# Relative-position-bias softmax: stores on ScalarE's queue, single-row first loads, one last store

## The chip, the cores and the metric

The kernel runs on one core of a Trainium2 chip. The metric is device time in microseconds (us) of one execution; the median of three runs before the change is 1330.56 us (1330.31 to 1331.54). The profile is of one further execution, taken by the hardware profiler.

## The reference

The input is a tensor of logits of shape (2, 8, 2112, 2112) in fp32 and, per head, a table of 33 biases. Each logit gets the bias of its clipped relative position, and each row goes through a softmax:

```python
rel = pos[:, None] - pos[None, :]
rel_clipped = np.clip(rel, -16, 16) + 16
logits = logits + rel_bias[:, rel_clipped][None]
logits = logits - logits.max(axis=-1, keepdims=True)
exp = np.exp(logits)
return exp / exp.sum(axis=-1, keepdims=True)
```

Input and output have 285.5 MB each, and every element is read once and written once.

## The kernel before

A row of the softmax has S = 2112 elements (8448 bytes). Rows are dealt to the 128 partitions so that one partition holds 33 consecutive rows of one head: 64 blocks of 33 rows make the 2112 rows of a head, and two heads fill the 128 partitions. Inside a partition the bias of a row is a window into one strip `F` of 2144 values, shifted by one place from row to row. `strip(k)` builds `F` from the bias table for a pair of heads.

The outer loop `k` runs over K = 4 pairs of heads. Inside it there are 12 chunks: two batches, each cut into chunks of 6, 5, 6, 5, 6 and 5 rows per partition. That makes 48 chunks over the whole run. Four buffers `X[0]` to `X[3]` (`NBUF`) of up to six rows hold chunks in turn, so chunk n uses buffer n mod 4, and it is loaded, computed in place, and stored from there.

The engines go through a chunk like this:

- `add` on VectorE (L167): per row, one instruction adds the strip's window and gives the negated row maximum. It waits for the chunk's load (`ld[b]`).
- `exps` on ScalarE (L175): per row, the exponential with its row sum.
- `scale`: VectorE takes the reciprocals of the sums (L183) and scales the first three rows (`DV = 3`, L187), counting `scaled`.
- `scale_rest` on ScalarE (L192) scales the other two or three rows, counting `scaledA`.

VectorE and ScalarE each run a hardware loop over `k` with the 12 chunks written out.

All transfers of logits and results are issued by SyncE (SP). `load` (L87) fetches a whole chunk, and `store` (L95) first waits until the chunk is scaled. The first four loads are issued at the start; from then on `turn` gives the order:

```python
store(k + n // NT, n % NT)
take(nc.sync, st[(n - 1) % NBUF], 16)
load(k + (n + 3) // NT, (n + 3) % NT)
```

So SP issues store n, waits until store n-1 has landed, and then issues load n+3 into the buffer that became free. All of these stand in one queue, loads and stores in turn. The last chunk is stored in two parts: its first three rows, which VectorE scales, and then its last two. The bias table (132 KB, L103) is the only transfer on ScalarE's queue; `strip` needs it.

Of the kernel before, what the change touches and what calls it, by code (L numbers as in the profile page):

```python
# [11 lines left out]
ENG = mybir.EngineType  # L12
# [3 lines left out]
def kernel(  # L16
# [6 lines left out]
    nc = tc.nc  # L23
    P = 128
    B, H, S, S2 = logits.shape
# [4 lines left out]
    K = H // 2  # L30
# [3 lines left out]
    NBUF = 4  # L34
    SIZES = [6, 5, 6, 5, 6, 5]
# [3 lines left out]
    CH = [(b, sum(SIZES[:i]), r) for b in range(B) for i, r in enumerate(SIZES)]  # L39
    NT = len(CH)  # L40
# [3 lines left out]
    X = [io.tile([P, R * S], FP32, tag=f"X{b}", name=f"X{b}") for b in range(NBUF)]  # L44
# [14 lines left out]
    def rows(t, k, m, s0, n):  # L59

        b, j, r = CH[m]
        return bass.AP(
            tensor=t.tensor,
            offset=t.offset + (b * H * S + j + s0) * S + k * (2 * S * S),
            ap=[[W * S, P], [1, n * S]],
        )

    with tc.tile_critical(no_gpsimd_drain=True):
        ld = [nc.alloc_semaphore(f"ld{b}") for b in range(NBUF)]
        st = [nc.alloc_semaphore(f"st{b}") for b in range(NBUF)]  # L70
        added = nc.alloc_semaphore("added")
        expd = nc.alloc_semaphore("expd")
        scaled = nc.alloc_semaphore("scaled")
        scaledA = nc.alloc_semaphore("scaledA")
        inv = nc.alloc_semaphore("inv")
        invA = nc.alloc_semaphore("invA")
        rb = nc.alloc_semaphore("rb")
        idx = nc.alloc_semaphore("idx")
        dve = nc.alloc_semaphore("dve")

        def take(eng, sem, n):
            eng.wait_ge(sem, n).then_inc(sem, -n)  # L82


        def load(k, m):
            b, r = m % NBUF, CH[m][2]
            nc.sync.dma_start(out=X[b][:, 0 : r * S], in_=rows(logits, k, m, 0, r)).then_inc(ld[b], 16)  # L87

        def store(k, m, s0=0, n=None):
            b, n = m % NBUF, n or CH[m][2]  # L90
            if s0 < DV:
                take(nc.sync, scaled, DV)
            if s0 + n > DV:
                take(nc.sync, scaledA, s0 + n - DV)
            nc.sync.dma_start(  # L95
                out=rows(out, k, m, s0, n), in_=X[b][:, s0 * S : (s0 + n) * S]
            ).then_inc(st[b], 16)

        for m in range(NBUF):
            load(0, m)  # L100

        rbB = view(F, 0, [[1, H * W]])
# [1 line left out]
            out=rbB,  # L104
            in_=bass.AP(tensor=rel_bias.tensor, offset=rel_bias.offset, ap=[[0, P], [1, H * W]]),
# [7 lines left out]
        v = nc.vector  # L113
# [23 lines left out]
        def strip(k):  # L137

            then(v.tensor_copy(out=rbK[:, :], in_=rbP[:, bass.ds(k, 1), :]))  # L139
            settle()  # L140
            low, high = rbK[:, W - 1 : W], rbK[:, 0:1]
            blocks = view(F, MR, [[W, NB], [1, W]])
            then(v.tensor_tensor(out=blocks, in0=view(eq, 0, [[1, NB], [0, W]]),  # L143
                                 in1=view(rbK, W - 1, [[0, NB], [-1, W]]), op=ALU.mult))
            then(v.tensor_scalar(out=rest, in0=lt, scalar1=low, scalar2=None, op0=ALU.mult))  # L145
            then(v.tensor_copy(out=F[:, 0:MR], in_=low.to_broadcast([P, MR])))  # L146
            then(v.tensor_copy(out=F[:, FW - MR : FW], in_=high.to_broadcast([P, MR])))  # L147
            settle()
            then(v.scalar_tensor_tensor(out=rest, in0=gt, scalar=high, in1=rest, op0=ALU.mult, op1=ALU.add))  # L149
            settle()  # L150
            then(v.tensor_tensor(out=blocks, in0=blocks, in1=view(rest, 0, [[1, NB], [0, W]]), op=ALU.add))  # L151
            settle()

        def row(m, i):
            return X[m % NBUF][:, i * S : (i + 1) * S]

        def col(t, m, i, n=1):
            c = m % NBUF * R + i
            return t[:, c : c + n]

        DV = 3

        def add(m):
            take(v, ld[m % NBUF], 16)
            j, r = CH[m][1:]
            for i in range(r):
                v.tensor_tensor_reduce(  # L167
                    out=row(m, i), in0=row(m, i), in1=F[:, W - 1 - j - i : W - 1 - j - i + S],
                    scale=-1.0, scalar=BIG, op0=ALU.add, op1=ALU.min, accum_out=col(nmax, m, i),
                ).then_inc(added, 1)  # L170

        def exps(m):
            for i in range(CH[m][2]):
                take(nc.scalar, added, 1)
                nc.scalar.activation(  # L175
                    out=row(m, i), in_=row(m, i), func=ACTF.Exp, scale=-1.0, bias=col(nmax, m, i),
                    accum_out=col(tot, m, i),
                ).then_inc(expd, 1)

        def scale(m):  # L180
            r = CH[m][2]
            take(v, expd, r)
            v.reciprocal(out=col(rec, m, 0, r), in_=col(tot, m, 0, r)).then_inc(inv, 1)  # L183
            v.wait_ge(inv, 1).then_inc(inv, -1)  # L184
            v.sem_inc(invA, 1)
            for i in range(DV):
                v.tensor_scalar_mul(out=row(m, i), in0=row(m, i), scalar1=col(rec, m, i)).then_inc(scaled, 1)  # L187

        def scale_rest(m):
            take(nc.scalar, invA, 1)  # L190
            for i in range(DV, CH[m][2]):
                nc.scalar.activation(  # L192
                    out=row(m, i), in_=row(m, i), func=ACTF.Copy, scale=col(rec, m, i),
                ).then_inc(scaledA, 1)

        with nc.Fori(0, K, 1, engines=[ENG.DVE]) as k:
            strip(k)
            for m in range(NT):
                add(m)
                scale(m)  # L200
        with nc.Fori(0, K, 1, engines=[ENG.Activation]):  # L201
            for m in range(NT):
                exps(m)
                scale_rest(m)

        def turn(k, first, stop):
            for n in range(first, stop):
                store(k + n // NT, n % NT)  # L210
                take(nc.sync, st[(n - 1) % NBUF], 16)
                load(k + (n + 3) // NT, (n + 3) % NT)

        store(0, 0)
        with nc.Fori(0, K - 1, 1, engines=[ENG.SP]) as k:
            turn(k, 1, NT + 1)
        turn(K - 1, 1, NT - 3)
        for m in range(NT - 3, NT - 1):
            store(K - 1, m)
        r = CH[NT - 1][2]  # L220
        store(K - 1, NT - 1, 0, DV)
        store(K - 1, NT - 1, DV, r - DV)
        for b in range(NBUF):
            take(nc.sync, st[b], 32 if b == (NT - 1) % NBUF else 16)


# [28 lines left out]
```

## Time and profile before

| | |
|---|---|
| median of three runs | 1330.56 us |
| profiled execution | 1330.28 us, span 1328.5 us |
| VectorE busy | 818.9 us (62%) |
| ScalarE busy | 808.8 us (61%) |
| moved by DMA | 571.13 MB, 430 GB/s over the span |
| share of 16 DMA engines' time on SP's queue | 99.7% |
| median from issue to landing, load of six / five rows | 39.7 / 42.1 us |
| median from issue to landing, store of six / five rows | 46.9 / 48.6 us |

The span runs from the first to the last recorded instruction. GB/s counts what the DMA engines moved in either direction, and a DMA share of 1.00 means that all 16 engines had a packet in hand all the time. A packet is counted where it falls, so rates of short windows waver by some per cent. "SPq" and "ACTq" are the sequencers of SyncE and ScalarE, on which the DMA issues stand; they are not counted as busy time.

### The profile page before, as it was taken

The numbers are of one execution on the slowest core, as the hardware profiler recorded it, in microseconds if no ns is written. First come the engines' busy times: TensorE is split into PE (matmuls) and PEld (weight loads), VectorE is DVE, ScalarE is ACT, GpSimd is POOL, SyncE is SP. The second block draws the span as 40 slices with busy tenths as digits, with TensorE's granted clock in tenths as the row PEclk, the third lists the DMA queues.
The fourth block names the chain that finished last, engine by engine and source line by source line (L and its number), as shares of the span: only waits on it lengthen the run. The fifth ranks groups of instructions, "written<-read, shape, count | busy, mean of one in ns | idle before, by whom it ended". The sixth has DMA issues, their size and how long they took to land. (4 is left out here: it accounts for less than half of the span.)

```text
span 1328.5 us, 2379 instructions
## 1 busy us (share of the span) xinstructions
DVE 818.9 (62%) x753; ACT 808.8 (61%) x652; POOL 0.6 (0%) x6
## 2 busy tenths in 40 slices
DVE  4885665557755566555866466664676547665572
ACT  2895575655756557555675566764667646675472
POOL 0000000000000000000000000000000000000000
DMA  9999999999999999999999999999999999999998
GB/s 390 436 426 427 427 434 429 430 429 439 432 435 429 431 442 428 439 430 429 440 431 438 428 432 435 437 436 428 430 431 445 429 424 436 434 431 430 435 433 371
DMA packets 14117, 571.13 MB, mean 430 GB/s; under 512 B 1568, under 2 KB 1696, under 8 KB 1696
## 3 DMA queue, kind: packets, MB, share of 16 engines
q1 hardware_dynamic: 13968, 570.96, 99.7%
q10 hardware_dynamic: 144, 0.14, 0.0%
q14 instruction: 5, 0.04, 0.0%
HBM read 285.61 MB, written 285.47 MB: 430 GB/s over the span
## 5 line engine op out<-in xcount | busy, mean ns | idle before, releaser
L167 DVE CUSTOM_DVE_ANT_0 X<-X,F 128x2112 f32<-128x2112 f32 x264 | 605.5, 2354 | 340.1 <-DVEq L82 340.1
L175 ACT ACTIVATE X<-X,nmax 128x2112 f32<-128x2112 f32 x264 | 542.2, 2054 | 407.4 <-ACTq L82 381.6
L192 ACT ACTIVATE X<-X,rec 128x2112 f32<-128x2112 f32 x120 | 238.8, 2046 | 29.0 <-ACTq L82 29.0
L187 DVE TENSOR_SCALAR X<-X,rec 128x2112 f32<-128x2112 f32 x144 | 181.4, 1316 | 12.4 <-DVEq L184 12.4
L183 DVE RECIPROCAL rec<-tot 128x6 f32<-128x6 f32 (+1 forms) x48 | 9.1, 190 | 116.1 <-DVEq L82 116.1
L175 ACT ACTIVATION_READ_ACCUMULATOR X<-X,nmax 128x1 f32 x264 | 49.2, 186 | 0.0
L175 ACT ACT_TABLE_LOAD x4 | 5.1, 1283 | 60.7 <-ACTq L82 60.7
L167 DVE DVE_READ_ACCUMULATOR2_ANT nmax<- 128x1 f32 x264 | 21.8, 83 | 0.0
L151 DVE TENSOR_TENSOR F<-F,rest 128x2112 f32<-128x2112 f32 x4 | 9.4, 2359 | 0.6
L143 DVE TENSOR_TENSOR F<-Z,rbK 128x2112 f32<-128x2112 f32 x4 | 9.4, 2358 | 0.6
L134 DVE COPY rbP<-F 64x132 f32<-64x132 f32 x2 | 0.4, 224 | 14.5 <-DMA F<-in_rel_bias_dram 14.4
L149 DVE SCALAR_TENSOR_TENSOR rest<-Z,rbK,rest 128x64 f32<-128x64 f32 x4 | 1.1, 284 | 0.6 <-DVEq L82 0.2
L128 DVE TENSOR_SCALAR Z<-F 128x64 f32<-128x64 f32 x3 | 0.5, 221 | 1.5 <-POOL F L108 1.5
L145 DVE TENSOR_SCALAR rest<-Z,rbK 128x64 f32<-128x64 f32 x4 | 1.1, 275 | 0.0
L139 DVE COPY rbK<-rbP 128x33 f32 x4 | 0.7, 176 | 0.3 <-DVEq L82 0.3
L147 DVE COPY F<-rbK 128x16 f32<-128x16 f32 x4 | 0.7, 167 | 0.0
L146 DVE COPY F<-rbK 128x16 f32<-128x16 f32 x4 | 0.7, 164 | 0.0
L108 POOL IOTA F<- 64x64 f32 x2 | 0.4, 178 | 0.7 <-PEq L250 0.6
L239 POOL MEMSET const-bfloat16-1.0<- 128x1 bf16 x1 | 0.1, 101 | 0.0
L239 POOL MEMSET const-float32-0.0<- 128x1 f32 x1 | 0.1, 98 | 0.2 <-issue 0.2
L239 POOL MEMSET const-float32-1.0<- 128x1 f32 x1 | 0.1, 98 | 0.0
L239 POOL MEMSET const-uint8-127<- 128x1 uint8 x1 | 0.1, 98 | 0.0
## 6 DMA issues: line engine op xcount, KB each, us to landing
X<-in_logits_dram SPq DMA_DIRECT2D x24, 6336.0 KB, 39.7
out_dram<-X SPq DMA_DIRECT2D x24, 6336.0 KB, 46.9
X<-in_logits_dram SPq DMA_DIRECT2D x24, 5280.0 KB, 42.1
out_dram<-X SPq DMA_DIRECT2D x23, 5280.0 KB, 48.6
out_dram<-X SPq DMA_DIRECT2D x1, 3168.0 KB, 16.6
out_dram<-X SPq DMA_DIRECT2D x1, 2112.0 KB, 21.1
F<-in_rel_bias_dram ACTq DMA_DIRECT2D x1, 132.0 KB, 15.5
```

What stands on the lines that cost most here:

```text
L139: then(v.tensor_copy(out=rbK[:, :], in_=rbP[:, bass.ds(k, 1), :]))
L143: then(v.tensor_tensor(out=blocks, in0=view(eq, 0, [[1, NB], [0, W]]), in1=view(rbK, W - 1, [[0, NB], [-1, W]]), op=ALU.mult))
L145: then(v.tensor_scalar(out=rest, in0=lt, scalar1=low, scalar2=None, op0=ALU.mult))
L146: then(v.tensor_copy(out=F[:, 0:MR], in_=low.to_broadcast([P, MR])))
L147: then(v.tensor_copy(out=F[:, FW - MR : FW], in_=high.to_broadcast([P, MR])))
L149: then(v.scalar_tensor_tensor(out=rest, in0=gt, scalar=high, in1=rest, op0=ALU.mult, op1=ALU.add))
L151: then(v.tensor_tensor(out=blocks, in0=blocks, in1=view(rest, 0, [[1, NB], [0, W]]), op=ALU.add))
L167: v.tensor_tensor_reduce(out=row(m, i), in0=row(m, i), in1=F[:, W - 1 - j - i : W - 1 - j - i + S], scale=-1.0, scalar=BIG, op0=ALU.add, o ...
L175: nc.scalar.activation(out=row(m, i), in_=row(m, i), func=ACTF.Exp, scale=-1.0, bias=col(nmax, m, i), accum_out=col(tot, m, i),).then_inc( ...
L183: v.reciprocal(out=col(rec, m, 0, r), in_=col(tot, m, 0, r)).then_inc(inv, 1)
L187: v.tensor_scalar_mul(out=row(m, i), in0=row(m, i), scalar1=col(rec, m, i)).then_inc(scaled, 1)
L192: nc.scalar.activation(out=row(m, i), in_=row(m, i), func=ACTF.Copy, scale=col(rec, m, i),).then_inc(scaledA, 1)
```

## The change

Three things change. Stores are issued by ScalarE, in its own queue, after the chunk's exps and scales; VectorE's and ScalarE's scaled rows are counted on one semaphore. SP issues loads only, each after the store that frees its buffer has landed. Chunk 0 is loaded by six DMAs of one row each; the first five count on a new semaphore `pre`, which VectorE awaits before its loop. The last chunk is stored by one DMA like the others.

```diff
-        def store(k, m, s0=0, n=None):
-            b, n = m % NBUF, n or CH[m][2]
-            if s0 < DV:
-                take(nc.sync, scaled, DV)
-            if s0 + n > DV:
-                take(nc.sync, scaledA, s0 + n - DV)
+        def store(k, m):
+            b, n = m % NBUF, CH[m][2]
+            take(nc.scalar, scaled, n)
+            nc.scalar.dma_start(
+                out=rows(out, k, m, 0, n), in_=X[b][:, 0 : n * S]
+            ).then_inc(st[b], 16)
+
+        r0 = SIZES[0]
+        for i in range(r0):
             nc.sync.dma_start(
-                out=rows(out, k, m, s0, n), in_=X[b][:, s0 * S : (s0 + n) * S]
-            ).then_inc(st[b], 16)
-
-        for m in range(NBUF):
+                out=X[0][:, i * S : (i + 1) * S], in_=rows(logits, 0, 0, i, 1)
+            ).then_inc(ld[0] if i == r0 - 1 else pre, 16)
+        for m in range(1, NBUF):
             load(0, m)
...
-                ).then_inc(scaledA, 1)
-
+                ).then_inc(scaled, 1)
+
+        take(v, pre, 16 * (r0 - 1))
         with nc.Fori(0, K, 1, engines=[ENG.DVE]) as k:
             strip(k)
             for m in range(NT):
                 add(m)
                 scale(m)
-        with nc.Fori(0, K, 1, engines=[ENG.Activation]):
+        with nc.Fori(0, K, 1, engines=[ENG.Activation]) as k:
             for m in range(NT):
                 exps(m)
                 scale_rest(m)
-        def turn(k, first, stop):
-            for n in range(first, stop):
-                store(k + n // NT, n % NT)
-                take(nc.sync, st[(n - 1) % NBUF], 16)
-                load(k + (n + 3) // NT, (n + 3) % NT)
-
-        store(0, 0)
+                store(k, m)
+
+        def reload(k, n):
+            take(nc.sync, st[n % NBUF], 16)
+            load(k + (n + NBUF) // NT, (n + NBUF) % NT)
+
         with nc.Fori(0, K - 1, 1, engines=[ENG.SP]) as k:
-            turn(k, 1, NT + 1)
-        turn(K - 1, 1, NT - 3)
-        for m in range(NT - 3, NT - 1):
-            store(K - 1, m)
-        r = CH[NT - 1][2]
-        store(K - 1, NT - 1, 0, DV)
-        store(K - 1, NT - 1, DV, r - DV)
+            for n in range(NT):
+                reload(k, n)
+        for n in range(NT - NBUF):
+            reload(K - 1, n)
         for b in range(NBUF):
-            take(nc.sync, st[b], 32 if b == (NT - 1) % NBUF else 16)
+            take(nc.sync, st[b], 16)
```

More of the change, by code (lines that the diff above doesn't have):

```diff
@@ L73 @@
         scaled = nc.alloc_semaphore("scaled")
-        scaledA = nc.alloc_semaphore("scaledA")
         inv = nc.alloc_semaphore("inv")
@@ L77 @@
         rb = nc.alloc_semaphore("rb")
+        pre = nc.alloc_semaphore("pre")
         idx = nc.alloc_semaphore("idx")
```

## The prediction

> **What bounds the kernel now.** I read the page from its second and third part, because its first already rules the engines out: VectorE and ScalarE are each busy for some 61% of the span. The slices and the queues say what is not idle:
>
> ```profile
> DMA  9999999999999999999999999999999999999998
> GB/s 390 436 426 427 427 434 429 430 429 439 432 435 429 431 442 428 439 430 429 440 431 438 428 432 435 437 436 428 430 431 445 429 424 436 434 431 430 435 433 371
> DMA packets 14117, 571.13 MB, mean 430 GB/s; under 512 B 1568, under 2 KB 1696, under 8 KB 1696
> q1 hardware_dynamic: 13968, 570.96, 99.7%
> ```
>
> The 16 DMA engines are busy in every slice, and SyncE's queue (q1) accounts for 99.7% of their time. Only the first and the last slice move clearly less. So the time is bytes over rate, and a change can act in four places only: the head, the tail, the rate, and a moment in which no transfer is queued. Next the table of windows (columns: stretch, its length, busy time of VectorE, ScalarE and GpSimd, clock, DMA share, GB/s):
>
> ```profile
> 4.00:14.00 10.00, 0.00 (x0) 0.00 (x0) 0.00 (x0) 1.00 1.00 409
> 57.00:84.00 27.00, 23.32 (x21) 22.98 (x19) 0.00 (x0) 1.00 1.01 436
> 84.00:104.00 20.00, 13.64 (x14) 15.22 (x13) 0.00 (x0) 1.00 1.01 413
> 104.00:250.00 146.00, 89.53 (x81) 88.78 (x72) 0.00 (x0) 1.00 1.00 429
> 250.00:500.00 250.00, 156.37 (x144) 152.40 (x124) 0.00 (x0) 1.00 1.00 434
> 1000.00:1280.00 280.00, 169.39 (x154) 172.72 (x139) 0.00 (x0) 1.00 1.00 433
> 1305.00:1328.50 23.50, 0.68 (x1) 0.93 (x1) 0.00 (x0) 1.00 0.79 342
> ```
>
> From 250 us on the rate stands at 433 to 434 GB/s. It is lower at 84:104, where the first loads and stores meet in the queue, and in the tail. Last, the timeline near the end, where the first add of a chunk marks the landing of its load:
>
> ```profile
> 1232.69 2.36 DVE L167 CUSTOM_DVE_ANT_0 X<-X,F 128x2112 f32<-128x2112 f32 x1 [6.92 <-DVEq L82]
> 1245.08 0.34 SPq L87 DMA_DIRECT2D X<-in_logits_dram  x1
> 1251.15 0.33 SPq L95 DMA_DIRECT2D out_dram<-X  x1
> 1260.12 2.36 DVE L167 CUSTOM_DVE_ANT_0 X<-X,F 128x2112 f32<-128x2112 f32 x1 [9.31 <-DVEq L82]
> 1282.80 24.45 SPq L95 DMA_DIRECT2D out_dram<-X  x3
> 1287.57 2.36 DVE L167 CUSTOM_DVE_ANT_0 X<-X,F 128x2112 f32<-128x2112 f32 x1 [7.07 <-DVEq L82]
> 1305.77 1.47 SPq L95 DMA_DIRECT2D out_dram<-X  x2
> ```
>
> Number the 48 chunks 0 to 47; even ones have six rows, odd ones five. Chunks 45, 46, 47 start 27.4 us apart, which is one load and one store of eleven rows in all: 11 x 2112 x 4 x 128 B = 11.9 MB at 434 GB/s. VectorE waits 7 to 9 us before each. Computing a chunk takes 18.5 us with five rows (1232.69 to 1251.15) and 22.7 us with six (1260.12 to 1282.80). At 1287.57 the last load is in; sixteen rows are then still to be stored, 17.3 MB or 39.9 us, and 1287.6 + 39.9 = 1327.5 is the end of the span within a microsecond. Before the last store can be issued (1305.77, 18.2 us on), the queue still has stores 45 and 46, 12.5 + 15.0 = 27.5 us. So the engines never run dry, with 9 us to spare.
>
> **The change part by part.** The profiled execution took 1330.28 us for a span of 1328.5, 0.28 below the median of 1330.56; sums on the span get 2.1 us added.
>
> *Single-row loads and the wait for them.* Five more DMAs go through SP's sequencer. Its first four issues took 2.07 us, 0.5 each, while one row (1.08 MB) takes 2.5 us to move, so issuing stays ahead. VectorE's new wait for rows 0 to 4 stands before the first strip; behind it wait the strip, all adds, and through them ScalarE. Five rows are 12.5 us of transfer, so the wait ends near 15 us. Now the strip begins at 17.2, held by the 132 KB table, which takes 15.5 us because its packets take turns with those of the loads (below). With shorter packets the table comes sooner, the strip starts at 15 to 16, and chunk 0 is 1 to 2 us early. That is worth nothing: the loads of chunks 0 to 3 (22 rows, 23.8 MB) fill the engines until about 57 us, and store 0 is issued at 46.27 already. Between +1 us (the head loses another tenth of its first 10 us) and -1 us, I take 0.
>
> A rule that speaks against this part is in the Trainium skill, "DMA: Bandwidth & Descriptors", section Bandwidth: make transfers 1 MiB or more, a single 1 MB copy reaching 341 GB/s where 16 MB reach 425. By it the six rows would take 19.0 us where the trace's rate gives 15.0, an estimate of +4 us; it counts transfers that start alone, and here five others are queued behind each, so I go by the trace.
>
> *Stores on ScalarE's queue.* 48 issues at 0.35 us (the rows of SP's timeline) are 17 us of ScalarE, against 407 us that it idles before its exps. The wait for all scaled rows stands behind ScalarE's own copies; VectorE's three scales (3.8 us) run beside those two or three (4.0 or 6.0 us), so it waits for nearly nothing. Queued behind it are the next chunk's exps, and behind those VectorE's reciprocal: 0.35 us more on 18.5 or 22.7, in a cadence of 27.4. Free, as long as the cadence is set by DMA.
>
> *SP's order.* Its turn was store n, wait for store n-1, load n+3; now it only waits for store n and loads n+4, the same dependency. Store 44 was issued at 1227.95 and chunk 44's scaling ended at 1227.9, so SP delayed no store. Removed: nothing on the path.
>
> *Two queues on the same engines.* This is the step that matters. The table's load shows how two queues share. Each DMA is 128 packets, one per partition, and 16 small ones (13968 = 97 x 144), so each engine has eight. Eight turns behind a six-row packet (50.7 KB at 27.1 GB/s per engine, 1.87 us) are 15.0 us; the table took 15.5. So the queues alternate packet by packet. A load and a store together then take what they took one after the other: 27.4 us. The buffer's cycle is 4 x 27.4 = 109.7; less some 30 for the load (27.4 and about 2.5 of issue and landing) and 18.5 or 22.7 of compute, 57 to 61 us are left for the store, which needs 27.4. So a second store is always queued and the engines are always fed.
>
> Does alternating cost rate? Upper bounds: 4:14, where the table's packets alternate with load 0, ran 25 GB/s under 434, or 0.58 us in 5.3 turns; 8 x 48 = 384 turns would cost 42 us. And 413 GB/s (84:104) for all 571 MB would cost 66 us. Lower bound: from 250 us on every engine changes from load to store each 12 to 15 us at 434, and nothing above 434 is held over such a stretch, so no gain from rate. I take 0, the row of most of the run and of full-size transfers; the upper end stays open.
>
> The Trainium skill, same page, section Rules for kernel authors, says that spreading DMAs over issuing engines brings no bandwidth, as all run on the same 16 engines; by it this step is 0. It doesn't say whether reads and writes mixed at every packet cost any.
>
> *One last store.* Store 47 needed 12.5 us in two parts. When load 47 lands at time 0, store 46 was issued at -27.4 + 22.7 = -4.7 and is whole behind store 45, itself issued at -36.4 and due at about +23: some 9 of its 12.5 us are left. 9 + 15.0 = 24 cover chunk 47's 18.5 us. The single store is issued when its second half was: 0.
>
> **Sum**: 1328.5 + 0 + 2.1 = 1330.6; I say 1331.
>
> **The rivals.**
> *Mixing costs rate.* For it: 413 at 84:104 and 429 at 104:250, where loads and stores first meet. Against: 434 later with the same changes of direction. At 429 the 571.13 MB take 1331.3 instead of 1317.5 us (433.5): +14, so 1344. *Heavily*, as in the two upper bounds: +42 to +66, 1372 to 1396.
> *The tail runs dry.* If stores get more than every second turn, the waiting moves from the store queue to the load queue, and at the last load's landing only store 46 is left: 15.0 - 2.3 = 12.7 us for 18.5 of compute. DMA idles 6 us: 1337; with nothing at all left, 18.5: 1349. It decides once fewer than 18.5 us of stores are queued there, where I count 24. Against it: the table's packets got just one turn in two.
> *Faster.* The tail at 342 instead of 434 lacks 5.0 us; the dips of 84:250 lack 2.6. If the finer mix spreads the engines' ends and meetings better, most of that returns: -4.5, 1326; at most -7.6, 1323. For it: the tail and the dips are there; against: no row says that they are due to the order.
>
> **How the numbers follow.** Forecast 0.34, mixing 0.25, heavy mixing 0.08, dry tail 0.13, faster 0.20. A measurement tells about 0.2% (2.7 us) from no change; the forecast's own spread puts 0.27 within, 0.02 below and 0.05 above. So faster 0.22, same 0.27, slower 0.51. The range runs from the faster case's bound, 1323, over mixing with half as much again (1351), leaving out the heavy case and a little: 1323 to 1352. The forecast alone: 1328 to 1334.
>
> **What would show it.** Right: DMA share 1.00 in all windows, 433 GB/s from 250 us on, loads landing 30 us after issue (now 39.7 and 42.1) and stores 57 to 61 (now 46.9 and 48.6), the first strip at 15 to 16 us. Mixing: share 1.00 at a lower rate in the middle. Dry tail: a low share between the last load's landing and store 47's issue, and loads slower than stores from issue to landing. Wrong in another way: a middle window with a share below 1.00, a moment with neither queue filled.

## The result, and the profile after

The changed kernel takes 1337.34 us (median of six runs, 1336.72 to 1339.49) against 1330.77 for the kernel before in the same runs: a ratio of 1.0051, 95% interval 1.0038 to 1.0064. It is slower by some 6.6 us, half a per cent. The profiled execution took 1338.30 us, with a span of 1336.5 us, 8.0 more than before.

The second and third part of its page, and its DMA issues (the last columns: KB of one DMA, median us from issue to landing):

```profile
DMA  9999999999999999999999999999999999999996
GB/s 384 433 440 426 436 434 432 438 435 431 431 434 431 434 430 434 432 439 435 429 435 428 434 434 433 432 429 432 433 436 427 433 434 432 431 432 429 436 416 279
...
q1 hardware_dynamic: 7632, 285.48, 49.7%
q10 hardware_dynamic: 7056, 285.61, 49.4%
...
out_dram<-X ACTq DMA_DIRECT2D x24, 6336.0 KB, 50.0
X<-in_logits_dram SPq DMA_DIRECT2D x23, 6336.0 KB, 37.8
X<-in_logits_dram SPq DMA_DIRECT2D x24, 5280.0 KB, 37.8
out_dram<-X ACTq DMA_DIRECT2D x24, 5280.0 KB, 54.3
```

The two queues now share the engines' time evenly, and up to the last two slices hardly anything is lost. The last slice is where the kernel got slower: 279 GB/s instead of 371, at a DMA share of six tenths. Windows of the kernel after (columns as before: stretch, its length, three engines' busy time, clock, DMA share, GB/s):

```profile
57.00:250.00 193.00, 126.16 (x115) 127.54 (x103) 0.00 (x0) 1.00 1.00 433
250.00:1280.00 1030.00, 630.39 (x576) 622.59 (x502) 0.00 (x0) 1.00 1.00 433
...
1294.00:1300.00 6.00, 0.04 (x1) 2.24 (x2) 0.00 (x0) 1.00 0.78 335
...
1305.00:1336.50 31.50, 10.70 (x10) 12.59 (x10) 0.00 (x0) 1.00 0.62 268
...
1312.00:1318.00 6.00, 3.62 (x4) 5.40 (x4) 0.00 (x0) 1.00 0.14 59
1318.00:1324.00 6.00, 0.35 (x1) 0.60 (x1) 0.00 (x0) 1.00 0.80 342
...
1330.00:1336.50 6.50, 0.00 (x0) 0.00 (x0) 0.00 (x0) 1.00 0.29 123
```

and of the kernel before:

```profile
57.00:250.00 193.00, 126.49 (x115) 126.99 (x103) 0.00 (x0) 1.00 1.00 428
250.00:1280.00 1030.00, 640.90 (x587) 634.66 (x513) 0.00 (x0) 1.00 1.00 433
...
1312.00:1318.00 6.00, 0.00 (x0) 0.00 (x0) 0.00 (x0) 1.00 0.94 407
```

The middle runs at 433 GB/s in both, and between 57 and 250 us the changed kernel is even faster. Between 1312 and 1318 us it has only 0.14 of the DMA engines at work: 0.14 x 16 = 2.2 engines. Before, it was 0.94. Summed over the tail, the mean engine is idle for 31.5 x 0.38 = 12.0 us from 1305 us on; before, the same sum was 23.5 x 0.21 = 4.9 us. The 7.1 us between them, with 1.3 us more at 1294:1300, are about the growth of the span.

What the engines wait for there stands in the timeline of the kernel after. The first line is the issue of load 47; the adds mark the landing of loads 46 and 47; the last two lines are stores 46 and 47:

```profile
1262.34 0.33 SPq L87 DMA_DIRECT2D X<-in_logits_dram  x1
...
1273.66 2.36 DVE L170 CUSTOM_DVE_ANT_0 X<-X,F 128x2112 f32<-128x2112 f32 x1 [10.28 <-DVEq L82]
...
1296.47 0.34 ACTq L92 DMA_DIRECT2D out_dram<-X  x1
1300.24 2.36 DVE L170 CUSTOM_DVE_ANT_0 X<-X,F 128x2112 f32<-128x2112 f32 x1 [6.20 <-DVEq L82]
...
1318.83 0.34 ACTq L92 DMA_DIRECT2D out_dram<-X  x1
```

Load 47 lands at 1300.2 instead of 1287.6. Chunk 47 takes its 18.6 us, and by then most engines have nothing left: that is the rival "the tail runs dry", with its 6 us. Two engines, though, still work through that gap: they are a second cause.

The trace holds one more reading that the experiments use. Every DMA ends with sixteen small packets, one for each engine, so the time between the first and the last of them tells how far the engines are apart. In one queue all engines work through the same list, and this spread is the lag of the slowest. In the kernel before it grows to 4.7 us by 260 us and stays about there to the end (4.6 at the last store). In the changed kernel it grows all the way: stores 1.0 us at first, 6.3 at 700 us, 22 at 1262 us; loads 0.8 at first, 6.3 at 690 us, 8.3 at load 47. With two queues the spreads of loads and of stores differ, so neither is the lag alone.

These completions also tell which of the two causes sets the end of the profiled execution. The slowest engine completes load 47 at 1299.6 us and stores 45, 46 and 47 at 1307.4, 1322.4 and 1334.9. The last two steps, 15.0 and 12.5 us, are what six and five rows take it, packet after packet, so this engine never paused. Fourteen engines had completed store 46 by 1312.8, waited some 7 us for store 47, and were done by 1332.4. So closing the gap alone could not have moved the end. The lag also widens the gap: load 47 was complete on the fourteen at 1291.4 to 1294.8, but chunk 47's computing had to wait for the two others.

### The profile page after: what moved, and what is told of

It is laid out like the page before. It is cut to its first block, busy times and chain, and to the rows that moved or that the text cites. A ratio compares the mean times of both kernels' runs of the same rounds, so it can differ in the third digit from the quotient of the medians.

```text
span 1336.5 us, 2391 instructions
## 1 busy us (share of the span) xinstructions
DVE 819.0 (61%) x753; ACT 808.3 (60%) x652; POOL 0.6 (0%) x6
## 5 line engine op out<-in xcount | busy, mean ns | idle before, releaser
L186 DVE RECIPROCAL rec<-tot 128x6 f32<-128x6 f32 (+1 forms) x48 | 9.1, 190 | 116.1 <-DVEq L82 116.1
## 6 DMA issues: line engine op xcount, KB each, us to landing
X<-in_logits_dram SPq DMA_DIRECT2D x23, 6336.0 KB, 37.8
X<-in_logits_dram SPq DMA_DIRECT2D x24, 5280.0 KB, 37.8
out_dram<-X ACTq DMA_DIRECT2D x24, 5280.0 KB, 54.3
```

## The experiments

Theory "dry tail": the time is lost because the store queue is empty while chunk 47 is computed. Its rivals at the start were "mixing" (a lower rate in the middle) and "head" (the single rows). After the first four runs a third joined, "lag": with two queues some engines fall behind, and the slowest sets the end.

**Chunk 0 by one DMA, in the changed kernel.**

```diff
-        for i in range(r0): ... one row each, counting ld[0] or pre
-        for m in range(1, NBUF):
+        for m in range(NBUF):
             load(0, m)
-        take(v, pre, 16 * (r0 - 1))
```

> The changed kernel with chunk 0 loaded by one DMA again and VectorE's extra wait gone; stores stay on ScalarE's queue. Theory 'dry tail' (the 6.6 us come from an end at which the store queue is empty while chunk 47 is computed): the head is not the cause, so 1336 to 1338 us, with the DMA share low again between the end of store 46 and the issue of store 47. Theory 'head' (single rows and the wait cost the time): 1331 us.

Measured: 1336.02 us, ratio 1.0034 (1.0021 to 1.0046). Most of the loss stays without the single rows. Its own runs scatter from 1333.35 to 1338.77.

**The single rows alone, in the kernel before.**

```diff
-        for m in range(NBUF):
+        for i in range(r0): ... one row each, counting ld[0] or pre
+        for m in range(1, NBUF):
             load(0, m)
+        take(v, pre, 16 * (r0 - 1))
```

> The kernel before with the single-row loads of chunk 0 and VectorE's wait for them alone. Theories 'dry tail' and 'mixing': 1330 to 1332 us, the DMA engines having loads 1 to 3 to move in any case. Theory 'head': 1335 us or more.

Measured: 1331.01 us, ratio 1.0000 (0.9991 to 1.0009). The head costs nothing, and "head" falls.

**One last store, in the kernel before.**

```diff
-        for m in range(NT - 3, NT - 1):
+        for m in range(NT - 3, NT):
             store(K - 1, m)
-        r = CH[NT - 1][2]
-        store(K - 1, NT - 1, 0, DV)
-        store(K - 1, NT - 1, DV, r - DV)
```

> The kernel before with chunk 47 stored by one DMA instead of two. The queue still holds 27.5 us of stores when load 47 lands, so all theories give no change: 1330 to 1331.5 us. If the split at the end mattered, 1333 us or more.

Measured: 1330.04 us, ratio 1.0002 (0.9993 to 1.0011). No change. What is left of the change is the queue that the stores stand in.

**The last three stores back behind load 47.** In the changed kernel ScalarE only signals that chunks 45 to 47 are done, and SP issues their stores after its last load.

```diff
+            if m < NT - 3:
                 store(K - 1, m)
+            else:
+                take(nc.scalar, scaled, CH[m][2])
+                nc.scalar.sem_inc(last, 1)
...
+        for m in range(NT - 3, NT):
+            take(nc.sync, last, 1)
+            nc.sync.dma_start(out=rows(out, K - 1, m, 0, n), ...)
```

> The changed kernel, but stores 45, 46 and 47 are issued by SP, in its queue behind load 47; all earlier ones stay on ScalarE's queue. Theory 'dry tail': load 47 no longer takes turns with store 45, lands some 10 us earlier, and finds 27.5 us of stores behind it for 18.5 us of compute, so DMA stays busy: 1329 to 1331 us. Theory 'mixing' (packets of loads and stores in turn lower the rate in the middle): the middle is unchanged, so 1336 to 1338 us. Theory 'head': 1336 to 1338 us too.

Measured: 1336.58 us, ratio 1.0036 (1.0024 to 1.0048), single runs from 1331.6 to 1337.6. The expectation failed. Windows of this kernel:

```profile
1312.00:1324.00 12.00, 0.73 (x1) 0.98 (x1) 0.00 (x0) 1.00 0.93 401
1324.00:1330.00 6.00, 0.00 (x0) 0.00 (x0) 0.00 (x0) 1.00 0.38 162
1330.00:1335.60 5.60, 0.00 (x0) 0.00 (x0) 0.00 (x0) 1.00 0.05 23
```

Load 47 lands 5.6 us earlier (not 10), and the gap before the last store is mostly gone: the share is 0.93 at 1312:1324, and most engines pause for 2.6 us, where they paused for some 7 in the changed kernel. Yet the end comes as late. Of store 47's sixteen completions fourteen come between 1326.5 and 1327.4 us, the last two at 1332.9 and 1334.0: the kernel waits for two stragglers. So a dry tail was there and was cut by two thirds, and the lag already stood at nearly the same end.

**The converse: only the last three stores on ScalarE's queue, in the kernel before.**

```diff
+            if m >= NT - 3:
+                ...
+                nc.scalar.dma_start(out=rows(out, K - 1, m, 0, n), ...)
...
-        for m in range(NT - 3, NT - 1):
-            store(K - 1, m)
-        store(K - 1, NT - 1, 0, DV)
-        store(K - 1, NT - 1, DV, r - DV)
```

> The converse: the kernel before, with stores 45, 46 and 47 alone moved to ScalarE's queue (47 as one store). Theory 'dry tail': store 45, issued at 1251, takes turns with the 9 us left of load 46, store 44 and load 47, all of which come 12.5 us later; load 47 lands at about 1300 instead of 1287.6, store 46 is then half done, and DMA idles some 6 us before store 47: 1336 to 1339 us. Theories 'mixing' and 'head': 1330 to 1331.5 us, since neither the middle nor the head is touched.

Measured: 1346.88 us, ratio 1.0122 (1.0108 to 1.0137), 16 us and not 6. The windows show a dry tail without a straggler at the last store (its completions lie within 0.2 us):

```profile
1306.00:1312.00 6.00, 0.53 (x1) 0.00 (x0) 0.00 (x0) 1.00 0.70 303
1312.00:1318.00 6.00, 6.00 (x5) 3.91 (x3) 0.00 (x0) 1.00 0.02 8
1318.00:1324.00 6.00, 4.96 (x6) 5.61 (x7) 0.00 (x0) 1.00 0.00 0
1324.00:1330.00 6.00, 3.97 (x4) 5.22 (x4) 0.00 (x0) 1.00 0.00 0
```

For nearly all of chunk 47's computing the DMA engines do nothing. I had store 46 half done when load 47 lands; it was issued at 1287.76, took turns with load 47 from then on, and they landed at 1311.3 (the load) and 1315.0 (the store), so next to nothing was left. This is the upper bound of the prediction's rival, 18.5 us of idling, and it shows that the dry tail is real where it occurs.

**How much the second queue costs by the number of chunks that use it.** The first 12, 24 or 36 stores go to ScalarE's queue; then everything is in SP's queue again in the old order, so that the end is that of the kernel before.

```diff
+        with nc.Fori(0, J, 1, engines=[ENG.Activation]) as k:
+            ... exps, scale_rest, store on ScalarE's queue
+        with nc.Fori(J, K, 1, engines=[ENG.Activation]):
+            ... exps, scale_rest
...
+        ... reload(k, n) up to the last of these chunks
+        turn(J - 1, NT, NT + 1)      # from here on the old order
```

> The kernel before, but the first 12 of the 48 stores are issued by ScalarE in its own queue; from chunk 12 on everything is in SP's queue in the old order. Theory 'lag' (while two queues feed the same engines, some engines fall behind the others a little with every chunk, and the slowest sets the end; stores 45 to 47 moved to SP left 5.6 us of loss for 45 chunks): a quarter of it, 1.5 us, less the 2.3 us that 433 instead of 428 GB/s gains between 57 and 250 us: 1329 to 1331 us. Theory 'dry tail alone': the end is the old one, so 1328 to 1330 us.

> The same with the first 24 stores on ScalarE's queue. Theory 'lag': half of 5.6 us, less the early gain: 1330 to 1333 us. Theory 'dry tail alone': 1328 to 1330 us.

> The same with the first 36 stores on ScalarE's queue, the last 12 chunks in the old order, long enough for the old backlog of stores to build up again. Theory 'lag': three quarters of 5.6 us or more, since the lag of single engines stays once it is there: 1333 to 1336 us. Theory 'dry tail alone': 1328 to 1330 us.

Measured, with the other runs of the series (the spreads are those of load 47 and of the last store in one profiled execution each; in the last two lines the last store's spread is small because the slow engines caught up during the gap; medians come from several sets of runs, so compare by the ratio):

| stores on ScalarE's queue | median us | ratio (95% interval) | spread of load 47, us | spread of the last store, us |
|---|---|---|---|---|
| 0 | 1330.77 | 1 | 4.5 | 4.6 |
| first 4 | 1330.06 | 0.9993 (0.9984 to 1.0002) | 5.3 | 5.2 |
| first 8 | 1329.35 | 0.9991 (0.9982 to 1.0000) | 5.2 | 5.6 |
| first 12 | 1328.95 | 0.9998 (0.9989 to 1.0007) | 5.3 | 5.2 |
| first 24 | 1330.86 | 1.0008 (1.0000 to 1.0017) | 8.3 | 7.8 |
| first 36 | 1334.23 | 1.0026 (1.0015 to 1.0036) | 11.4 | 7.8 |
| first 45, the rest behind load 47 | 1336.58 | 1.0036 (1.0024 to 1.0048) | 12.8 | 7.5 |
| all 48, chunk 0 whole | 1336.02 | 1.0034 (1.0021 to 1.0046) | 11.0 | 1.3 |
| all 48, the changed kernel | 1337.34 | 1.0051 (1.0038 to 1.0064) | 8.3 | 2.7 |

From 24 chunks on the loss grows with the number of chunks on two queues, although those kernels end in the old single queue; up to 12 chunks there is none. "Dry tail alone" would have left 36 stores at 1328 to 1330 us; they took 1334.23. The spread goes with it. With 36 stores on the second queue, the last of these lands at 1040 us with a spread of 15.8 us, the load before it with 9.9; from then on there is one queue, and the spread is 11.5 us at 1047 us and still at 1062, 1171 and 1281 us. In that stretch of one queue the lag is neither made nor made good (the kernel before did make its 4.7 us in one queue, before 260 us). The tail of this kernel ends like the one above:

```profile
1312.00:1324.00 12.00, 0.00 (x0) 0.00 (x0) 0.00 (x0) 1.00 0.99 425
1324.00:1330.00 6.00, 0.00 (x0) 0.00 (x0) 0.00 (x0) 1.00 0.34 146
1330.00:1334.40 4.40, 0.00 (x0) 0.00 (x0) 0.00 (x0) 1.00 0.10 42
```

A third of the engines work at 1324:1330, and three are left after it, the last until 1332.9 us; that one completed load 47 and the stores after it without a pause, as in the changed kernel. A lag that differs from run to run would also explain why runs scatter more, 1328.7 to 1337.2 with 36 stores where the kernel before stays within 1329.2 and 1331.5; with one trace for each kernel that isn't shown.

**Packets of one row in the stores, then in the loads.** Both change the changed kernel with chunk 0 loaded whole.

```diff
-            nc.scalar.dma_start(out=rows(out, k, m, 0, n), in_=X[b][:, 0 : n * S])
+            for i in range(n):
+                nc.scalar.dma_start(out=rows(out, k, m, i, 1), in_=X[b][:, i * S : (i + 1) * S])
```

> The changed kernel with chunk 0 loaded whole, and every store issued as one DMA per row (8.4 KB packets) where loads keep packets of five or six rows. Theory 'turns' (the two queues take turns packet by packet, whatever their size): loads get six times the bytes of stores while both queues are filled, land some 20 us after issue instead of 40, and the waiting moves into the store queue, so that whole stores 45 and 46 are left when load 47 lands and DMA doesn't idle before the last store. What is then left is the lag of single engines: 1330 to 1335 us. If turns are by bytes: landings as before and 1336 us.

> The opposite: every load issued as one DMA per row, stores whole. Theory 'turns': stores land some 20 us after issue, loads 65 to 70 us, and at the landing of load 47 at most store 46 is left in part: DMA idles 8 us or more before store 47, 1339 to 1346 us. If turns are by bytes: 1336 us.

Measured: 1367.67 us, ratio 1.0295 (1.0278 to 1.0313), with rows in the stores, and 1355.32 us, ratio 1.0193 (1.0179 to 1.0207), with rows in the loads. On who gets the engines both came out as "turns" has it; the DMA issues of the first:

```profile
X<-in_logits_dram SPq DMA_DIRECT2D x24, 6336.0 KB, 23.7
X<-in_logits_dram SPq DMA_DIRECT2D x24, 5280.0 KB, 21.1
```

and of the second:

```profile
out_dram<-X ACTq DMA_DIRECT2D x24, 6336.0 KB, 21.9
out_dram<-X ACTq DMA_DIRECT2D x24, 5280.0 KB, 20.3
```

The queue with the larger packets lands in 20 to 24 us instead of 40 to 52 (the kernel with chunk 0 whole): the queues take turns by packet, not by byte. The packet records show it directly: while both queues hold work, an engine moves one packet of the one, then one of the other, whatever their sizes. In the changed kernel 99% of the successions that can be told apart between 100 and 1280 us alternate so. On the time both expectations failed, the first by far. Rows in the loads gave the dry tail (a share of 0.40 at 1310:1320) and, beyond it, a rate of 427 GB/s from 57 to 1250 us. Rows in the stores ran at 423 GB/s from 57 to 1250 us, and ScalarE got stuck at its own issues. Of its 264 store issues 83 took more than 1 us, the longest 14.9, and its DMA issues took 435 us in all, against 17 in the changed kernel. One of them in its timeline, of 11.4 us (the second column):

```profile
1240.10 11.40 ACTq L92 DMA_DIRECT2D out_dram<-X  x1
```

and in its waits VectorE's reciprocal, which needs the exps behind such issues, waited 497.3 us in total instead of 116.1:

```profile
DVE rec L181 <- DVEq L81: 497.3, 48, 19.6
```

So as a cure for the tail this was worse than the ailment. It doesn't show what the lag alone costs.

**Fewer stores on the second queue.** The first 4 or 8 stores only, since between 57 and 250 us two queues had gained 5 GB/s.

```diff
+            if m < 8:
+                store_act(0, m)
...
+        for n in range(8 - 1):
+            reload(0, n)
...
+        turn(0, 8, NT + 1)
```

> The kernel before with the first 4 stores on ScalarE's queue, the rest in SP's old order (until about 150 us). If the dip of the rate between 84 and 250 us comes from the first meetings of loads and stores in one queue, some 1 us of it is saved, and no lag has built up: 1328 to 1330 us, against 1330 for the kernel before. If the dip only moves to where the queue becomes a single one: 1330 to 1331 us.

> The same with the first 8 stores (until about 260 us), which covers the whole dip: 1328 to 1329.5 us where the gain of 2 us holds and the lag of 8 chunks is 1 us or less; 1330 to 1331 us where the dip only moves.

Measured: 1330.06 us and 1329.35 us, ratios 0.9993 (0.9984 to 1.0002) and 0.9991 (0.9982 to 1.0000), in the table above. With 8 stores the rate at 57:250 is 432 GB/s, with 4 it is 429, before it is 428. The sign is that of a gain of 1 us, but one interval holds 1 and the other ends on it. I don't count either as a faster kernel.

## Why the prediction was right or wrong

**The time and the sign.** 1337.34 us lies in the range of 1323 to 1352 and on the slower side, which had 0.51. The single forecast of 1331 was not what happened. The rival "the tail runs dry" had 1337 for the case with only store 46 left, and that gap is in the profile. But the agreement of the number is partly luck: there are two causes whose ends lie within 3 us of each other (1332.4 and 1334.9 in the trace), and the rivals named only the one that ends first. The rival's own reason didn't occur either: stores did not get more than every second turn, since the packets alternate one to one.

**Single rows and VectorE's wait: worth 0, right** (ratio 1.0000; the +4 us that the prediction weighed against it did not come). One term in it was off: the table did come sooner, 6.2 us after issue instead of 15.5, but the wait for five rows ended at 18.3 us and not at 15, so the strip began 1.1 us later than before instead of 1 to 2 earlier. The cover held: the loads of chunks 1 to 3 kept the engines busy.

**ScalarE's issues and its wait: worth 0, right.** 48 issues at 0.34 us; the wait for scaled rows shows nowhere.

**Rate of two queues: taken as 0, right.** The alternation packet by packet is as worked out. 433 GB/s in both kernels from 250 to 1280 us; the lower bound was the true one, and the row of full-size packets the right one to go by. The rival "mixing" has no evidence as a loss of mean rate. A price of small packets, however, does show where packets of one row meet packets of five or six all the time: 423 and 427 GB/s, less of a loss than the 409 of 4:14.

**The cover at the end: wrong, and this is the step that failed.** The prediction gave a load 30 us from issue to landing and a store 57 to 61, which put the waiting into the store queue and left 24 us of stores at the last landing. Measured were 37.8 for loads and 50.0 and 54.3 for stores. The missing term is a load's wait behind the load before it: load 47 was issued at 1262.34, while load 46 landed at 1273.66, 11 us later. What a load waits more, a store waits less: the buffer's cycle was right (37.8 + 22.7 + 50.0 and 37.8 + 18.5 + 54.3 are both some 110.5, where 109.7 was worked out), only its division was wrong. What sets this division is not shown. Store 45, due at +23 us after load 47's landing, was complete on fourteen engines 2 to 6 us before it and on the slowest 7 us after it. So on most engines some 12 us of store 46 were left instead of 24, under the 18.5 that are needed. Store 46's issue, 3.8 us before the landing, was as worked out (4.7).

**"The engines are always fed" took the sixteen engines for one.** The DMA share of 1.00 in all middle windows was right, but it is a mean, and it doesn't tell that single engines fall behind. The tail of the kernel before, whose missing 5.0 us the prediction put under the rival "faster", is of the same kind: its engines end 4.6 us apart. The hope of that rival, that two queues would bring the engines closer, is the opposite of what happened: 8.3 us of spread at load 47 against 4.5. On the slowest engine the cover at the end did hold, and it still came last; no term of the prediction stood for that.

**What is shown and what is open.** Shown: the queue is what costs, the loss grows with the number of chunks on two queues, a spread built up there stays in the single queue after it, removing most of the gap before the last store doesn't remove the loss, and in the profiled execution the engine that ends last never paused in the tail. Not shown is why single engines fall behind. In the trace of the changed kernel a six-row load packet takes 1.880 us in the mean and a store packet 1.873, with a median of 1.872 for both, so slow packets are mostly reads; what slows them on some engines was not tried. How the 6.6 us divide between the lag and the gap is open too, as the gap itself is in part the lag's work: without the two slow engines load 47 would have landed some 5 us earlier (1294.8 instead of 1299.6, an estimate from the completions), and most of the pause would have gone with it.

## What to carry to other kernels

Where DMA is the bound and a change of queues leaves the rate alone, it is won or lost at the ends, but what is lost there can have built up all along. Work out what is left in the queues when the last load lands, by the measured time from issue to landing and with a load's wait for the load before it. A mean share over sixteen engines hides stragglers; the sixteen completions of one DMA show them. Here two queues took turns by packet, so the sizes of their packets decided which one waited, and one queue in a fixed order kept the engines closer together than two.

## What the runs showed of the hardware that I had not expected

- The lag of the engines is kept: 11.5 us of spread at 1062 us was 11.5 us at 1281 us in a single queue, while with a queue for stores of their own the spread of stores grew from 1 to 22 us over 1200 us and that of loads from 0.8 to 8.3.
- A queue of many small DMAs can stop the engine that issues it: with stores of one row each one issue took up to 14.9 us on ScalarE, against 0.34 us for stores of whole chunks, and with loads of one row up to 20.0 us on SyncE.
- Packets of 8.4 KB beside packets of 42 to 51 KB lowered the rate from 433 to 423 GB/s (small stores) and 427 GB/s (small loads), while six such loads at the head cost nothing that could be measured.
